# The low halves of the feature-major weights move within their 512-byte frame: 64 bytes in the attention part, 320 in the feed-forward part

## The chip, the cores and the metric

The kernel runs on one core of a Trainium2 chip. The metric is the device time of one execution in microseconds (us), lower is better. Before the change three runs took 1100.12, 1100.26 and 1100.33 us, the median is 1100.26.

Engine names as in the profile: PE is TensorE, PEld its weight loads, DVE VectorE, ACT ScalarE, POOL GpSimd, SP the queue that issues most transfers.

## The reference

One layer of a streaming encoder on 256 tokens of width 2048, all in float32. Only the projections matter here:

```python
def hybrid_mixer(h, w_in_l, ...):
    proj = h @ w_in_l                       # 2048 x 6152
    ...                                     # eight forgetting-attention heads, eight stick-breaking heads
    return merged @ w_out_l                 # 2048 x 2048

def conv_ffn(h, w_up_l, conv_w_l, conv_b_l, w_down_l):
    u = h @ w_up_l                          # 2048 x 11264
    ...                                     # causal depthwise convolution over 3 tokens, split in gate and val
    return (jax.nn.silu(gate) * val) @ w_down_l      # 5632 x 2048
```

## The kernel before

**Three products for one.** The kernel keeps float32 accuracy by splitting each operand into a high part (rounded to the matmul's reduced format, F32R) and a low part (the rest), and adds three products: high times high, high times low, low times high. Weights stream from memory in tiles of 128 x 2048 floats (w_raw). `split` (L217) turns each into w_hi with a copy on ACT (L229) and w_lo with a subtraction on DVE (L232). Tokens are split once and stay: hT[k] holds, for 128 features, 256 high columns and then 256 low columns, so one row of hT[k] is 512 floats, 2048 bytes.

**Two ways to multiply.** A matmul on PE has a stationary operand of 128 x 128, brought in by a weight load, and a moving operand that streams past it. In the *token-major* products (`in_three`, L246, used by `token_major`, `in_seven`, `down_in_seven`; `down_plain` has a loop of its own) the tokens are stationary and the weights move. In the *feature-major* products (`from_features`, L275) it is the other way round: a block of 128 x 128 of the weights is stationary and the tokens move. There a weight tile holds eight blocks of rows and two of columns, so it gives 16 high products and 16 low ones:

```python
hi[:, i, j * P : (j + 1) * P], hT[k].rearrange("p a b -> p (a b)")    # high: 512 moving columns
lo[:, i, j * P : (j + 1) * P], hT[k][:, 0, :]                         # low: the 256 high columns of the tokens
```

`feature_major` (L297) does this for queries and keys of the stick-breaking heads (8 column groups of two halves each), `up_pieces` (L1160) for the whole up-projection (44 column groups of two halves each). That makes 104 weight tiles and 1664 low products. In the attention part and in the first part of the feed-forward layer the second half of a column group does its low products first, so that two groups of 16 low products meet there.

**Addresses.** Every tile has a fixed place in the core's memory, the same in all 128 partitions. One stationary block is 128 floats, 512 bytes, of a partition; the blocks of a feature-major weight tile lie 512 bytes apart and those of the tokens 2048. So within a group of products the place of weights and tokens modulo 512 never changes. In the program as built, hT stands at 96 modulo 512. The pools of w_hi and w_lo of the attention part (two buffers each for w_hi and w_lo) stand at 352, those of the feed-forward part (three each) at 96. Below, *distance* is the address of the stationary operand minus that of the moving one, modulo 512: in the feature-major products it is 256 in the attention part and 0 in the feed-forward part, for high and low alike.

**What sets the order.** PE, DVE, ACT, SP and POOL run the feed-forward layer in an order that is written by hand (L1346): transfers are issued 6 steps ahead of the matmuls, sums 4, splits 2. In the attention part only PE's order is by hand; weights are loaded and split with a raised priority (`weights`, L239).

Of the kernel before, what the change touches and what calls it, by code (L numbers as in the profile page):

```python
# [10 lines left out]
F32R = mybir.dt.float32r  # L11
# [4 lines left out]
P = 128  # L16
# [30 lines left out]
def hybrid_layer(  # L47
# [160 lines left out]
    def load(src):  # L208
        raw = wraw.tile([P, 2048], F32, name="w_raw", tag="w_raw")
        a, b = src.shape[1:]  # L210
        loaded.append(nc.sync.dma_start(raw[:, : a * b].rearrange("p (a b) -> p a b", a=a), src))
        return raw
# [1 line left out]
    loaded = []  # L214
    ordered, last_split = [False], []

    def split(raw, a, b):  # L217

        raws = raw if isinstance(raw, list) else [raw]
        hi = whi.tile([P, 2048], F32R, name="w_hi", tag="w_hi")  # L220
        lo = wlo.tile([P, 2048], F32R, name="w_lo", tag="w_lo")
        n = a * b
        m = n // len(raws)
        with ExitStack() as turn:
            for ins in last_split if ordered[0] else ():
                turn.enter_context(tc.issue_after(ins.ins))
            for i, r in enumerate(raws):
                some = slice(i * m, (i + 1) * m)
                copied = act.copy(hi[:, some], r[:, :m])  # L229
            for i, r in enumerate(raws):  # L230
                some = slice(i * m, (i + 1) * m)
                rest = dve.tensor_tensor(lo[:, some], r[:, :m], f32(hi[:, some]), op=ALU.subtract)  # L232
        last_split[:] = [copied, rest]
        return (
            hi[:, :n].rearrange("p (a b) -> p a b", a=a),
            lo[:, :n].rearrange("p (a b) -> p a b", a=a),
        )

    def weights(src, a, b):  # L239
        with tc.high_priority(offset=AHEAD):  # L240
            return split(load(src), a, b)

    def rows_of(w, k0, n, c0, cols):
        return w[k0 * P : (k0 + n) * P, c0 : c0 + cols].rearrange("(k p) c -> p k c", p=P)
# [30 lines left out]
    def from_features(acc, parts, kh, n=8, low_first=False):  # L275

        hi, lo = parts

        def high(k, i, j):
            nc.tensor.matmul(  # L280
                acc[:, j, :], hi[:, i, j * P : (j + 1) * P],
                hT[k].rearrange("p a b -> p (a b)"), start=k == 0, stop=low_first and k == KT - 1,
            )

        def low(k, i, j):
            nc.tensor.matmul(  # L286
                acc[:, j, S:], lo[:, i, j * P : (j + 1) * P], hT[k][:, 0, :],
                start=False, stop=not low_first and k == KT - 1,
            )

        for i0 in range(0, 8, n):
            for product in (low, high) if low_first else (high, low):
                for i in range(i0, i0 + n):
                    for j in range(2):
                        product(8 * kh + i, i, j)

    def feature_major(w, c0, pool, tag):  # L297

        acc = pool.tile([P, 2, 512], F32, name="pu", tag=tag)
        for kh in range(2):  # L300
            from_features(acc, weights(rows_of(w, 8 * kh, 8, c0, 2 * P), 8, 2 * P), kh, low_first=kh == 1)
            step()
        return acc

# [8 lines left out]
    with ExitStack() as actx:  # L313
# [6 lines left out]
        wlo = actx.enter_context(tc.tile_pool(name="wlo", bufs=2))  # L320
# [102 lines left out]
        def opening():  # L423

            acc = psa.tile([P, NT, 512], F32, name="acc", tag="acc")
            pairs = [[(0, 1), (1, 1)]] + [[(0, 2)]] * 7
            raws, parts = [], []

            def load_w(c, which=None, queue=nc.sync):

                if c == len(raws):
                    raw = wraw.tile([P, 2048], F32, name="w_raw", tag="w_raw")
                    raws.extend([raw[:, :1024], raw[:, 1024:]])
                for i, n in [(which, 1)] if which is not None else [(0, 2)]:
                    queue.dma_start(
                        raws[c][:, i * 512 : (i + n) * 512].rearrange("p (a b) -> p a b", a=n),
                        rows_of(wi, 2 * c + i, n, 0, 512),
                    )

            def split_w(c):  # L440
                hi = whi.tile([P, 2048], F32R, name="w_hi", tag="w_hi")
                lo = wlo.tile([P, 2048], F32R, name="w_lo", tag="w_lo")
                parts.append([t[:, :1024].rearrange("p (a b) -> p a b", a=2) for t in (hi, lo)])
                for i, n in pairs[c]:
                    cols = slice(i * 512, (i + n) * 512)
                    if c == i == 0:
                        dve.tensor_copy(hi[:, cols], raws[c][:, cols])
                        for k in range(2):
                            transposed_split(k, ga, 1)
                    elif c == 1:  # L450
                        for j in range(2):
                            half = slice(512 * j, 512 * (j + 1))
                            dve.tensor_copy(hi[:, half], raws[c][:, half])
                        transposed_split(2, ga)
                    else:
                        act.copy(hi[:, cols], raws[c][:, cols])
                    dve.tensor_tensor(
                        lo[:, cols], raws[c][:, cols], f32(hi[:, cols]), op=ALU.subtract
                    )

            def multiply(c, i, n, high):
                hi, lo = (p[:, i : i + n] for p in parts[c])
                order = [(j, l, hi) for j in range(n) for l in range(2)] if high else [(j, 0, lo) for j in range(n)]
                for m, (j, l, r) in enumerate(order):
                    for t in range(NT):
                        nc.tensor.matmul(
                            acc[:, t, :], of_half(hT[2 * c + i + j], l, t), r[:, j, :],
                            start=high and c == i == m == 0, stop=not high and c == 7 and m == n - 1,
                        )

            load_x(0, 2)
            nc.scalar.dma_start(prow[:KT, :], attn_norm[0].rearrange("(n p) -> n p", p=P))
            act.preload_act_table_set("natural_log_exp_and_others")
            load_w(0, 0)
            load_w(0, 1, nc.scalar)
            load_x(2, 2)
            load_w(1, 0, nc.scalar)
            load_w(1, 1)
            load_x(4, 2)
            load_w(2)  # L480
            load_x(6, 2)
            load_w(3)
            load_x(8, 4)
            load_w(4)
            load_x(12, 4)
            load_w(5)
            keep_busy(14)
            columns(ga, prow[:KT, :], KT)
            split_w(0)
            keep_busy(4)  # L490

            def behind(c):
                if c:
                    transposed_split(2 * c + 2, ga)
                split_w(c + 1)

            multiply(0, 0, 1, True)
            multiply(0, 1, 1, True)
            behind(0)
            sums_of_squares(ss1, 0, [0])  # L500
            multiply(0, 0, 1, False)
            multiply(0, 1, 1, False)
            for c in range(1, 8):
                if c < 7:
                    behind(c)
                sums_of_squares(ss1, c // 2, [c % 2])
                if c == 2:
                    load_w(6)
                    load_w(7)
                multiply(c, 0, 2, True)  # L510
                multiply(c, 0, 2, False)
            return acc
# [647 lines left out]
    def up_pieces(part, f0, follows):  # L1160

        c0 = f0 * P + (DFF if follows is val_follows else 0)
        cell = []

        def piece(kh):
            mem = {}

            def loads():
                mem["raw"] = load(rows_of(wu, 8 * kh, 8, c0, 2 * P))

            def prepare():
                mem["parts"] = split(mem["raw"], 8, 2 * P)

            def matmuls():
                if kh == 0:
                    cell.append(psa.tile([P, 2, 512], F32, name="pu", tag="acc"))
                from_features(cell[0], mem["parts"], kh, 8 if c0 else 4, kh == 1 and part.f_lo == 0)

            new_step(loads, None, prepare, matmuls, (lambda: follows(part, cell[0], f0)) if kh else None)

        piece(0)
        yield
        piece(1)
        yield
# [226 lines left out]
```

## Time and profile before

| | |
|---|---|
| time of the runs, median | 1100.26 us |
| the profiled execution's own time | 1099.91 us |
| its span, first to last instruction | 1098.0 us |
| mean granted TensorE clock | 1.000 |
| PE busy | 1092.8 us (100%) |
| PE weight loads busy | 947.6 us (86%) |
| DVE busy | 907.2 us (83%) |
| ACT busy | 721.6 us (66%) |
| high feature-major products (L280) | 1664 |
| low feature-major products (L286) | 1664 |

The span is taken from one profiled execution; the 1.9 us between the span and that execution's time lie outside the first and last instruction. Matmuls are pipelined: a record begins when a product begins and lasts until its last result is out, so records of neighbours overlap, and the time that a product costs is the step from its beginning to the next one's beginning, not its recorded length. A row of the timeline gives the beginning of the first of a merged group and the length until the last one ends; the group's cost is the distance between its beginning and that of the next row.

### The profile page before, as it was taken

How to read it: one execution, taken by the hardware profiler on the slowest of the kernel's cores; microseconds unless marked ns; L12 is line 12 of the kernel's file. 1: busy time of each engine (PE TensorE's matmuls, PEld its weight loads, DVE VectorE, ACT ScalarE, POOL GpSimd, SP SyncE). 2: the span in 40 equal slices, each digit the busy share in tenths (PEclk: the TensorE clock that was granted, in tenths of full speed). 3: DMA queues.
4: the chain of work that ended last, by engine and by line, in shares of the span. 5: the costliest groups of instructions: out<-in, count | busy, mean ns of one | idle time of the engine just before them, and what ended most of it. 6: DMA issues, size and time to landing. Idle time of an engine off the chain costs nothing. (4 is left out here: it accounts for less than half of the span.)

```text
span 1098.0 us, 14881 instructions
## 1 busy us (share of the span) xinstructions
PE 1092.8 (100%) x5844; PEld 947.6 (86%) x5844; DVE 907.2 (83%) x972; ACT 721.6 (66%) x929; POOL 52.8 (5%) x52
## 2 busy tenths in 40 slices
PE   9999999999999999999999999999999999999998
PEld 7998888888888888888888888888888888888887
DVE  5867877877789786789888988889798889889896
ACT  6756565664665566767767776677677677667753
POOL 0020000000000000001010000100000010100010
PEclk9999999999999999999999999999999999999999
DMA  8797655676649396558999697977979698987985
GB/s 289 232 271 222 191 154 153 197 241 202 207 124 288 118 318 192 187 180 229 278 233 273 194 268 260 260 257 181 326 200 314 197 229 267 263 266 186 320 212 171
DMA packets 182575, 251.15 MB, mean 229 GB/s; under 512 B 4528, under 2 KB 120650, under 8 KB 182250
## 3 DMA queue, kind: packets, MB, share of 16 engines
q1 hardware_dynamic: 162474, 209.67, 57.8%
q0 software_dynamic: 19712, 40.01, 19.7%
q8 instruction: 46, 0.75, 0.3%
q10 hardware_dynamic: 320, 0.53, 0.1%
q14 instruction: 23, 0.19, 0.0%
HBM read 248.08 MB, written 2.11 MB: 228 GB/s over the span
## 5 line engine op out<-in xcount | busy, mean ns | idle before, releaser
L232 DVE TENSOR_TENSOR w_lo<-w_raw,w_hi 128x2048 fp32r<-128x2048 f32 (+1 forms) x192 | 431.8, 2252 | 106.6 <-ACT w_hi L229 106.0
L229 ACT CAST w_hi<-w_raw 128x2048 fp32r<-128x2048 f32 (+1 forms) x192 | 360.9, 1882 | 212.3 <-PE pu L280 59.8
L280 PE MATMUL pu<-hT,w_hi 128*128 128x512 f32 x1664 | 394.0, 390 | 0.0
L280 PEld LDWEIGHTS pu<-hT,w_hi 128*128 128x128 f32 x1664 | 310.3, 188 | 63.1
L286 PEld LDWEIGHTS pu<-hT,w_lo 128*128 128x128 f32 x1664 | 211.9, 191 | 7.0
L286 PE MATMUL pu<-hT,w_lo 128*128 128x256 f32 x1664 | 215.2, 283 | 0.0
L254 PE MATMUL acc<-w_hi,hT 128*128 128x512 f32 (+1 forms) x512 | 113.5, 374 | 0.0
L254 PEld LDWEIGHTS acc<-w_hi,hT 128*128 128x128 f32 x512 | 91.5, 188 | 14.2
L232 DVE TENSOR_TENSOR w_lo<-w_sum,w_hi 128x2048 fp32r<-128x2048 f32 (+1 forms) x38 | 84.2, 2216 | 20.2 <-ACT w_hi L229 20.1
L229 ACT CAST w_hi<-w_sum 128x2048 fp32r<-128x2048 f32 (+1 forms) x38 | 70.3, 1850 | 45.0 <-PE pu L280 35.9
L1106 ACT ACTIVATE tap<-up,ccol 128x256 f32<-128x256 f32 x176 | 74.6, 495 | 0.0
L254 PE MATMUL acc<-w_lo,hT 128*128 128x512 f32 (+1 forms) x256 | 58.9, 372 | 0.0
L1211 POOL DMA_DIRECT2D w_sum<-in_w_down_dram x20 | 25.7, 1283 | 677.6 <-DVE w_lo L232 663.3
L254 PEld LDWEIGHTS acc<-w_lo,hT 128*128 128x128 f32 x256 | 46.4, 188 | 7.5
L254 PE MATMUL bank_a<-w_hi,g 128*128 128x512 f32 x160 | 40.1, 392 | 0.1
L254 PE MATMUL bank_b<-w_hi,s 128*128 128x512 f32 x160 | 40.0, 392 | 0.0
L254 PE MATMUL bank_a<-w_hi,s 128*128 128x512 f32 x160 | 40.0, 392 | 0.0
L254 PEld LDWEIGHTS bank_a<-w_hi,g 128*128 128x128 f32 x160 | 28.8, 189 | 5.8 <-issue 0.5
L254 PEld LDWEIGHTS bank_a<-w_hi,s 128*128 128x128 f32 x160 | 28.9, 189 | 5.3
L254 PEld LDWEIGHTS bank_b<-w_hi,s 128*128 128x128 f32 x160 | 28.9, 189 | 5.2
L1111 DVE TENSOR_TENSOR gate<-gate,tap 128x512 f32<-128x512 f32 x44 | 30.3, 689 | 2.5 <-ACT tap L1106 0.2
L1111 DVE TENSOR_TENSOR val<-val,tap 128x512 f32<-128x512 f32 x44 | 30.3, 689 | 2.3
(282 smaller groups left out, 1166.5 us busy)
## 6 DMA issues: line engine op xcount, KB each, us to landing
w_raw<-in_w_up_dram SPq DMA_DIRECT2D x88, 1024.0 KB, 6.8
w_raw<-in_w_down_dram SPq DMA_DIRECT2D x44, 1024.0 KB, 7.1
w_raw<-in_w_in_dram SPq DMA_DIRECT2D x36, 1024.0 KB, 5.5
w_sum<-in_w_down_dram POOLq DMA_DIRECT2D x20, 1024.0 KB, 9.7
w_raw<-in_w_out_dram SPq DMA_DIRECT2D x14, 1024.0 KB, 5.4
w_raw<-in_w_down_dram POOLq DMA_DIRECT2D x10, 1024.0 KB, 14.8
w_raw<-in_w_in_dram SPq DMA_DIRECT2D x10, 688.0 KB, 4.4
w_raw<-in_w_in_dram SPq DMA_DIRECT2D x6, 512.0 KB, 7.0
```

The source lines that it names most:

```text
L229: copied = act.copy(hi[:, some], r[:, :m])
L232: rest = dve.tensor_tensor(lo[:, some], r[:, :m], f32(hi[:, some]), op=ALU.subtract)
L254: nc.tensor.matmul(o, lhs(i, l, t), r[:, i, :], start=starts and j == 0, stop=stops and j == 3 * n - 1, skip_group_check=more,)
L280: nc.tensor.matmul(acc[:, j, :], hi[:, i, j * P : (j + 1) * P], hT[k].rearrange("p a b -> p (a b)"), start=k == 0, stop=low_first and k == ...
L286: nc.tensor.matmul(acc[:, j, S:], lo[:, i, j * P : (j + 1) * P], hT[k][:, 0, :], start=False, stop=not low_first and k == KT - 1,)
L1106: act.activation(taps[w][:, j, :], u[:, j, w : w + S], AF.Copy, scale=ccol[:, w, f : f + 1])
L1111: dve.tensor_tensor(a, a, tap, op=ALU.add)
L1211: nc.gpsimd.dma_start(mem[into][:, : nk * 512].rearrange("p (a b) -> p a b", a=nk), src, accum_op=ALU.add)
```

## The change

The buffers of w_lo grow from 2048 to 2176 columns (from 8192 to 8704 bytes, 16 and 17 times 512), and `split` takes a start column within them. The attention part's feature-major products ask for column 16 (64 bytes), the up-projection for column 80 (320 bytes); all other users stay at column 0. Since 8704 is a multiple of 512, every other buffer of the kernel keeps its address modulo 512. The low weights of the feature-major products then stand at 416 in both parts, which is a distance of 320 from the tokens at 96. Their high weights stay at distances of 256 and 0. The program has the same instructions in the same order on each engine, with the same waits; what differs is the address that DVE writes for w_lo and that PE reads for it.

```diff
+    LO_COLS = 2048 + 128
+
-    def split(raw, a, b):
+    def split(raw, a, b, lo0=0):
...
-        lo = wlo.tile([P, 2048], F32R, name="w_lo", tag="w_lo")
+        lo = wlo.tile([P, LO_COLS], F32R, name="w_lo", tag="w_lo")[:, lo0:]
...
-    def weights(src, a, b):
+    def weights(src, a, b, lo0=0):
         with tc.high_priority(offset=AHEAD):
-            return split(load(src), a, b)
+            return split(load(src), a, b, lo0)
...
-            from_features(acc, weights(rows_of(w, 8 * kh, 8, c0, 2 * P), 8, 2 * P), kh, low_first=kh == 1)
+            from_features(acc, weights(rows_of(w, 8 * kh, 8, c0, 2 * P), 8, 2 * P, 16), kh, low_first=kh == 1)
...
-                lo = wlo.tile([P, 2048], F32R, name="w_lo", tag="w_lo")
+                lo = wlo.tile([P, LO_COLS], F32R, name="w_lo", tag="w_lo")
...
-                mem["parts"] = split(mem["raw"], 8, 2 * P)
+                mem["parts"] = split(mem["raw"], 8, 2 * P, 80)
```

## The prediction

> **What bounds the kernel now.** I read first the page's busy times, then who PE waited for, then the timeline of one feature-major weight tile, then the recorded lengths of the products that the change touches, and last the other products in the kernel whose operands stand at other distances.
>
> The page's first part, busy time, share of the span and instructions, and from its fifth part the two groups of feature-major products (busy time, mean length of a record, idle time before them):
>
> ```profile
> span 1098.0 us, 14881 instructions
> PE 1092.8 (100%) x5844; PEld 947.6 (86%) x5844; DVE 907.2 (83%) x972; ACT 721.6 (66%) x929; POOL 52.8 (5%) x52
> ...
> L280 PE MATMUL pu<-hT,w_hi 128*128 128x512 f32 x1664 | 394.0, 390 | 0.0
> ...
> L286 PE MATMUL pu<-hT,w_lo 128*128 128x256 f32 x1664 | 215.2, 283 | 0.0
> ```
>
> PE is busy throughout, and neither group of products has idle time before it. The list of waits on PE is just this (in total, times, longest, in us):
>
> ```profile
> PE idle L419 <- DVE zeros L409: 1.1, 1, 1.1
> PE acc L466 <- ACT hT L154: 0.2, 1, 0.2
> ```
>
> PE waits 1.3 us in all, both times at the start. The kernel is therefore bound by the rate at which PE gets through its products; a nanosecond per product is paid or gained in full. In the stretch from 440 to 1050 us (us, then busy time of PE, its weight loads, DVE, ACT and POOL, granted clock, share of the transfer engines, GB/s):
>
> ```profile
> 440.00:1050.00 610.00, 610.00 (x3288) 530.01 (x3287) 533.85 (x474) 429.88 (x481) 34.90 (x27) 1.00 0.85 243
> ```
>
> DVE is free for 610.0 - 533.9 = 76 us of it and ACT for 180, so the engines that feed PE have a margin. The timeline of one weight tile (beginning, length, engine, line):
>
> ```profile
> 516.48 3.79 PE L280 MATMUL pu<-hT,w_hi 128*128 128x512 f32 x16
> 520.11 2.08 PE L286 MATMUL pu<-hT,w_lo 128*128 128x256 f32 x16
> 522.02 0.40 PE L254 MATMUL bank_a<-w_hi,s 128*128 128x512 f32 x1
> ```
>
> From beginning to beginning, 16 high products took 520.11 - 516.48 = 3.63 us, 227 ns each, and 16 low ones 522.02 - 520.11 = 1.91 us, 119 ns each. The low products in all take about 1664 x 119.4 = 199 us, 18% of the time. Their recorded lengths (shortest, median, longest in ns, weight loads first):
>
> ```profile
> L286 PEld LDWEIGHTS pu<-hT,w_lo x1664: 187/192/193, 152.3 to 1049.7; 128*128 128x128 f32 x185
> L286 PE MATMUL pu<-hT,w_lo x1664: 277/283/365, 152.6 to 1049.8; 128*128 128x256 f32 x185
> ```
>
> The median, 283, goes with the steady step of 120 ns. The shortest, 277, is that of the first product of a group, whose step is 113. A longer stall shows in the record one for one, so I use differences of recorded lengths as differences of steps.
>
> **The change, part by part.** *What goes and comes.* No instruction: order and waits are the same on all five engines. 242 writes of w_lo on DVE and the reads of w_lo on PE get new addresses; modulo 512 only those of the 104 feature-major tiles, 104 writes and 1664 products, are new. Larger buffers shift what lies behind them by multiples of 512; no wait changes by it.
>
> *The writes on DVE.* No row shows a write of w_lo at 416. The group is
>
> ```profile
> L232 DVE TENSOR_TENSOR w_lo<-w_raw,w_hi 128x2048 fp32r<-128x2048 f32 (+1 forms) x192 | 431.8, 2252 | 106.6 <-ACT w_hi L229 106.0
> ```
>
> I take no cost. The cover is DVE's 76 idle us between 440 and 1050 us: of the 104 writes 88 belong to the up-projection and most of them lie there, so each would have to grow by some 0.9 us, 40% of its 2.25, before PE waited. A write that gets shorter gains nothing either.
>
> *The 1664 low products.* The only term of the sum is their step at distance 320 in place of 0 and 256. These two are alike: at distance 256, in the attention part, sixteen took 154.48 - 152.57 = 1.91 us as well.
>
> ```profile
> 152.57 2.07 PE L286 MATMUL pu<-hT,w_lo 128*128 128x256 f32 x16
> 154.48 0.28 PE L793 MATMUL ps_o<-pT,vA 128*128 128x256 f32 x1
> ```
>
> The nearest row has the same shape, 256 moving columns, the same kind of data, and exactly this distance: in the attention heads L793 multiplies vA, stationary at 160 modulo 512, with pT, moving at 352, and 160 - 352 is 320 modulo 512. vB and vBlo stand at 224, so their distance is 384:
>
> ```profile
> L793 PE MATMUL ps_o<-pT,vA x24: 277/281/369, 134.1 to 206.6; 128*128 128x256 f32 x24
> ...
> L793 PE MATMUL ps_o<-w,vB x16: 274/284/367, 230.6 to 323.6; 128*128 128x256 f32 x16
> ...
> L793 PE MATMUL ps_o<-w,vBlo x8: 281/284/285, 230.9 to 323.7; 128*128 128x256 f32 x8
> ```
>
> At distance 320 the median is 281, against 283: 2 ns less. (The long ones of each group follow another kind of product and are not steady.) The timeline says the same of three in a row, 134.49 - 134.14 = 0.35 us, 117 ns each:
>
> ```profile
> 134.14 0.52 PE L793 MATMUL ps_o<-pT,vA 128*128 128x256 f32 x3
> 134.49 0.27 PE L794 MATMUL ps_o<-pT,vA_rest 128*128 128x128 f32 x1
> ```
>
> Against this speak products of another shape, 344 moving columns, where the weights move and summed tokens are stationary at 352. Rows of weights there begin 1376 bytes apart, so the distance changes within one tile. The mean over two products at the first row (weights at 352, distance 0), and two at the third (weights at 32, distance 320), around 87.7 and 88.3 us:
>
> ```profile
> L254 PE MATMUL bank_a<-w_hi,hT_sums 128*128 128x344 f32 x2 | 0.5, 316 | 0.0
> ```
>
> ```profile
> L254 PE MATMUL bank_a<-w_hi,hT_sums 128*128 128x344 f32 x2 | 0.5, 321 | 0.0
> ```
>
> Here distance 320 costs 5 ns more than distance 0. So the bounds for a low product are 277 - 283 = -6 ns below (the shortest that a low product itself shows) and +5 ns above. I take -2, from the row with the same number of columns, the same roles and the same distance; its weakness is that only three such products ever follow each other, where the change has 16.
>
> *Skill against row.* The Trainium skill says in "SBUF — State Buffer", section "Who interferes with whom", that TensorE has two read ports, one for the moving operand and one for weights, and that "PE and ACT never wait on anyone"; by that no address matters and the sum is 0. The two rows above, 316 and 321 ns for products that differ in nothing but their addresses, do not fit it.
>
> *The sum.* About 100 of the 1664 products open a group with a record of 277 already; at 281 they lose 4 ns, 0.4 us. The other 1564 gain 2 ns, 3.1 us. Net -2.7 us on the profiled execution's own 1099.91 us, 1097.2. The runs' median is 0.35 us above that execution, so the forecast is 1097.5 us. PE does not wait for DVE or ACT sooner by it: a tile's 16 low products shrink by 0.03 of 1.91 us.
>
> **The rivals.**
>
> *Nothing changes (address has no part in it).* For it: distances 0 and 256 give the same step. Against it: 316 and 321. Time: 1100.3. It is also what the Trainium skill's rule above would give. That the change does not do what it says is excluded by the addresses of the built program.
>
> *The stall goes for all 16.* The first product of each group shows that 256 columns can follow each other at 277 ns of record; if 320 keeps that up, 1564 products gain 6 ns, 9.4 us: 1090.9; with steps of 113 against 120 for them, 10.9 us, 1089.4. For it: the weight loads in the steady low groups are 192 ns long, 4 longer than the median of 188 in the vA row below, so something there holds both streams up. Against it: the vA row itself stays at 281.
>
> ```profile
> L793 PEld LDWEIGHTS ps_o<-pT,vA x24: 187/188/192, 133.9 to 206.4; 128*128 128x128 f32 x24
> ```
>
> *Slower: the weight load runs into the moving stream.* The reads of the next weights fall on the same part of the memory as those of the moving tokens, not at once but some way into the product, and hold them up for longer, as in the 344-column rows. It decides as soon as the step of a steady low product passes 120 ns. At the whole 5 ns the loss is 1664 x 5 = 8.3 us, 1108.6; at half of it 4.2 us, 1104.4. For it: same distance, same engine, and long runs. Against it: the other rows in that tile begin at other places too, and the roles are exchanged.
>
> **How the numbers follow.** A measurement of this kernel can tell about 0.2%, 2.2 us, from no change. Forecast 0.38: since its 2.7 us lie close to that bound, I put 0.25 of it on faster and 0.13 on within. Stall gone 0.20, faster. Nothing 0.14, within. Slower 0.28. Faster 0.45, within 0.27, slower 0.28. The range goes from 1089.4, the stall gone, to 1107.0, which leaves out the upper part of the slower case (about 0.13) and a little below. The forecast's own range, with 1 to 3 ns in place of 2, is 1096.0 to 1098.7.
>
> **What would show it.** Right: the median record of the low products falls from 283 to about 281, that of their weight loads from 192 to 188, sixteen of them take 1.88 to 1.89 us in the timeline, the high products keep 227 ns and 390, PE still waits 1.3 us. Wrong: a median of 283 (nothing), of 277 (stall gone) or of 285 and above (slower). It would also be wrong if the products that follow a low group changed their step; I leave these at nothing, since their own distances stay.

## The result and the profile after

The kernel after takes 1097.27 us (median of 8 runs, 1096.45 to 1098.09); the kernel before took 1100.34 us beside it (8 runs, 1099.83 to 1101.19). The ratio is 0.9971, with a 95% interval from 0.9961 to 0.9982: 0.29% faster, 0.18 to 0.39%. The forecast was 1097.5 us, the range 1089.4 to 1107.0.

The page of the kernel after, the lines that answer to those shown of before (all lines of the code stand two further down, so L288 is the low product and L282 the high one):

```profile
span 1094.7 us, 14881 instructions
PE 1089.0 (99%) x5844; PEld 944.8 (86%) x5844; DVE 907.0 (83%) x972; ACT 721.8 (66%) x929; POOL 52.8 (5%) x52
...
L282 PE MATMUL pu<-hT,w_hi 128*128 128x512 f32 x1664 | 393.9, 390 | 0.0
...
L288 PE MATMUL pu<-hT,w_lo 128*128 128x256 f32 x1664 | 212.2, 282 | 0.0
```

PE's busy time went down by 3.8 us and the span by 3.3. PE waits 1.9 us, where it was 1.3, all of it before the first moved product. DVE and ACT did the same work in the same time, so the write of w_lo at its new place cost nothing that shows. Recorded lengths of the low products' weight loads and of the products (shortest, median, longest):

```profile
L288 PEld LDWEIGHTS pu<-hT,w_lo x1664: 187/188/193, 152.5 to 1046.8; 128*128 128x128 f32 x185
L288 PE MATMUL pu<-hT,w_lo x1664: 275/282/369, 152.7 to 1046.9; 128*128 128x256 f32 x185
```

The weight loads' median fell from 192 to 188 ns, that of the products from 283 to 282. The same place in the program as in the prediction, sixteen low products and what follows them:

```profile
519.01 2.05 PE L288 MATMUL pu<-hT,w_lo 128*128 128x256 f32 x16
520.90 2.00 PE L256 MATMUL bank_a<-w_hi,s 128*128 128x512 f32 x8
522.74 1.07 PE L256 MATMUL bank_a<-w_lo,s 128*128 128x512 f32 x4
```

From beginning to beginning 520.90 - 519.01 = 1.89 us, where it was 1.91. The eight products behind them take 522.74 - 520.90 = 1.84 us, as before:

```profile
522.02 2.00 PE L254 MATMUL bank_a<-w_hi,s 128*128 128x512 f32 x8
523.86 1.07 PE L254 MATMUL bank_a<-w_lo,s 128*128 128x512 f32 x4
```

Ten nanoseconds are too coarse for steps that differ by two, so for the comparisons below I add up the step from the beginning of each PE record to the next, over three kinds of products: all 1664 low ones; the eight products that follow each low group, of whatever kind; and the high ones that are not among those eight. In us:

| kernel | distance of low / high | low | next eight | other high | span |
|---|---|---|---|---|---|
| before | 0, 256 / 0, 256 | 199.37 | 170.85 | 328.68 | 1098.0 |
| after | 320 / 0, 256 | 196.31 | 170.93 | 328.61 | 1094.7 |

The low products gained 199.37 - 196.31 = 3.06 us, which is the change of the span but for 0.24. The other two kinds moved by less than 0.1 us.

### The profile page after: what moved, and what is told of

It is laid out like the page before. It is cut to its first block, busy times and chain, and to the rows that moved or that the text cites. A ratio compares the mean times of both kernels' runs of the same rounds, so it can differ in the third digit from the quotient of the medians.

```text
span 1094.7 us, 14881 instructions
## 1 busy us (share of the span) xinstructions
PE 1089.0 (99%) x5844; PEld 944.8 (86%) x5844; DVE 907.0 (83%) x972; ACT 721.8 (66%) x929; POOL 52.8 (5%) x52
## 4 chain that ended last, share of the span: by engine, by line
PE 99%; DMA 0%; DVE 0%; SPq 0%; issue 0%
PE pu L282 35%; PE acc L256 19%; PE pu L288 18%; PE bank_a L256 12%; PE bank_b L256 6%; PE bank_c L256 3%; PE acc L468 2%; PE acc L1291 1%; PE ps_x L149 1%; PE ps_o L795 1%; PE bank_a L1291 1%; PE ps_p L811 0%; DMA w_raw<-in_w_in_dram 0%; PE ps_o L796 0%; PE ps_h L335 0%; PE ps_s L562 0%
## 5 line engine op out<-in xcount | busy, mean ns | idle before, releaser
L282 PE MATMUL pu<-hT,w_hi 128*128 128x512 f32 x1664 | 393.9, 390 | 0.0
L282 PEld LDWEIGHTS pu<-hT,w_hi 128*128 128x128 f32 x1664 | 310.4, 188 | 62.9
L288 PEld LDWEIGHTS pu<-hT,w_lo 128*128 128x128 f32 x1664 | 209.0, 189 | 6.8
L288 PE MATMUL pu<-hT,w_lo 128*128 128x256 f32 x1664 | 212.2, 282 | 0.0
```

The source lines that it names most:

```text
L282: nc.tensor.matmul(acc[:, j, :], hi[:, i, j * P : (j + 1) * P], hT[k].rearrange("p a b -> p (a b)"), start=k == 0, stop=low_first and k == ...
L288: nc.tensor.matmul(acc[:, j, S:], lo[:, i, j * P : (j + 1) * P], hT[k][:, 0, :], start=False, stop=not low_first and k == KT - 1,)
```

## The experiments

The theory, argued and not seen directly in any trace: each weight load reads its 512 bytes while the tokens of the product before it still stream past, and how often the two hold each other up depends on their distance. Rivals: the place of w_lo itself counts, not its distance from the tokens; or the larger buffers count; or the gain belongs to any place other than 0 and 256. Twelve kernels were run. Each but the last had one run, beside one of the kernel before, and a profile; the table holds what their profiles show.

| kernel | distance of low / high | low | next eight | other high | span | run, beside before |
|---|---|---|---|---|---|---|
| pad_only | 0, 256 / 0, 256 | 199.37 | 170.84 | 328.68 | 1098.9 | 1100.91, 1100.28 |
| all32 | 320 / 0, 256 | 196.31 | 170.94 | 328.61 | 1095.0 | 1097.00, 1099.89 |
| d64 | 64 / 0, 256 | 196.32 | 170.94 | 328.61 | 1095.2 | 1097.11, 1100.28 |
| d192 | 192 / 0, 256 | 196.31 | 172.91 | 328.79 | 1098.1 | 1100.16, 1100.28 |
| d288 | 288 / 0, 256 | 197.16 | 172.09 | 329.52 | 1097.6 | 1099.67, 1099.89 |
| d336 | 336 / 0, 256 | 197.59 | 172.45 | 329.51 | 1099.8 | 1101.62, 1100.42 |
| d352 | 352 / 0, 256 | 195.77 | 170.79 | 328.87 | 1094.8 | 1096.78, 1100.42 |
| d384 | 384 / 0, 256 | 200.35 | 169.52 | 329.20 | 1098.2 | 1100.23, 1100.28 |
| hi320 | 0, 256 / 320 | 199.13 | 171.50 | 338.06 | 1107.4 | 1109.42, 1099.89 |
| hi384 | 0, 256 / 384 | 199.10 | 171.17 | 337.81 | 1107.8 | 1109.88, 1100.42 |
| tm_low | 320 / 0, 256 | 196.31 | 170.94 | 329.89 | 1099.9 | 1101.89, 1099.89 |
| tail384 | 320, last four 384 / 0, 256 | 196.40 | 170.37 | 328.67 | 1094.5 | 1096.39, 1100.00 |

The first feature-major product begins between 148.7 and 150.1 us in these kernels, and none but tm_low changes a distance so far forward; single times and spans therefore carry more than 1 us that has nothing to do with the distance, and the sums of steps are the better measure.

### The larger buffers alone, and the distance kept at another place

pad_only keeps the 2176 columns and puts every user at column 0:

```diff
-            from_features(acc, weights(rows_of(w, 8 * kh, 8, c0, 2 * P), 8, 2 * P, 16), kh, low_first=kh == 1)
+            from_features(acc, weights(rows_of(w, 8 * kh, 8, c0, 2 * P), 8, 2 * P, 0), kh, low_first=kh == 1)
...
-                mem["parts"] = split(mem["raw"], 8, 2 * P, 80)
+                mem["parts"] = split(mem["raw"], 8, 2 * P, 0)
```

> The larger low buffers alone, all at column 0, so distances 0 and 256 as before. If the distance is the cause, everything is as before: 283 ns of record, 120 ns per steady low product, a span of 1098 us. If the larger buffers (what lies behind them moved by 512 to 1536 bytes) bring the gain, 281 ns and 1095 us.

```profile
L288 PEld LDWEIGHTS pu<-hT,w_lo x1664: 187/192/193, 153.6 to 1050.9; 128*128 128x128 f32 x185
L288 PE MATMUL pu<-hT,w_lo x1664: 277/283/365, 153.8 to 1051.0; 128*128 128x256 f32 x185
```

192 and 283 again, as before, and the same three sums within 0.01 us. The buffers' size is not the cause. The span of pad_only is 0.9 us above that of before; its first low product begins at 153.8 us, where before it was 152.6, so this comes from the opening.

all32 moves everything behind the constants by 32 bytes, tokens and weights together:

```diff
+    const.tile([P, 8], F32, name="pad32")
```

> The kernel after, with everything from the constants on moved by 32 bytes: tokens at 128 modulo 512, low weights at 448, every distance as in the kernel after. If the distance is the cause, nothing changes: 118 ns per low product, 227 per high one, a span of 1094.7 us. If the place itself matters (tokens that begin on a multiple of 64 bytes, or weights at 416), the steps of low and high products change.

```profile
L289 PEld LDWEIGHTS pu<-hT,w_lo x1664: 187/188/192, 152.3 to 1046.6; 128*128 128x128 f32 x185
L289 PE MATMUL pu<-hT,w_lo x1664: 276/281/369, 152.5 to 1046.7; 128*128 128x256 f32 x185
```

Same sums as the kernel after, 196.31, 170.94 and 328.61: the low weights stand at 448 here, the tokens at 128, and only relative places are the same. So a relative place is the cause, and the rival of the place itself has fallen. all32 keeps the low weights' distance to the high ones as well as to the tokens; hi320 below changes the first alone (w_hi goes from 96 or 352 to 416, w_lo stays) and leaves the low products at 199.13 us, against 199.37 before. So it is the distance from the tokens that counts.

### Other distances for the low weights

These differ from the kernel after in the two start columns alone:

```diff
# start columns of w_lo in the attention part and in the up-projection
-    16, 80      # after, 320
+    80, 16      # d64
+    112, 48     # d192
+    8, 72       # d288
+    20, 84      # d336
+    24, 88      # d352
+    32, 96      # d384
```

> Low feature-major weights at distance 64 from the tokens, not 320. If the loads and the moving tokens meet in a memory that repeats every 256 bytes (distances 0 and 256 were alike, 120 ns), a steady low product keeps the 118 ns that it has at 320, and the span stays near 1094.7 us. If only the distance modulo 512 counts, or the low weights' own place (416), the step may be anything between 113 and 126 ns: 113 would take 8 us off, 126 would add 13.

d64 gives 196.32, 170.94 and 328.61, the kernel after to 0.01 us. With 0 and 256 alike before, this is the second pair 256 apart that agrees; for these products the distance counts modulo 256.

> Distance 192. If any distance other than 0 and 256 gives what 320 gives: 118 ns, 1094.7 us. If the low weights must be read just ahead of the tokens, as at 64 and 320, this place, where the tokens are 64 bytes ahead modulo 256, should lose the gain: 120 ns or more, 1098 us or more.

Both answers were half right. The low products have exactly the gain of 320, 196.31 us. But the span is that of before, since the products behind the group pay for it, 172.91 against 170.85 us in the next eight and about 1 us more in products still further on, which the table does not hold. The timeline of d192, and then of the eight behind a group in d384:

```profile
519.45 2.05 PE L288 MATMUL pu<-hT,w_lo 128*128 128x256 f32 x16
521.33 2.03 PE L256 MATMUL bank_a<-w_hi,s 128*128 128x512 f32 x8
523.20 1.08 PE L256 MATMUL bank_a<-w_lo,s 128*128 128x512 f32 x4
```

```profile
520.59 2.08 PE L288 MATMUL pu<-hT,w_lo 128*128 128x256 f32 x16
522.51 1.99 PE L256 MATMUL bank_a<-w_hi,s 128*128 128x512 f32 x8
524.33 1.07 PE L256 MATMUL bank_a<-w_lo,s 128*128 128x512 f32 x4
```

The sixteen take 1.88 us at 192 and 1.92 at 384; the eight behind them, whose operands stand the same in all these kernels, take 1.87 and 1.82 us, where before and after have 1.84. Their single steps, from the records' beginnings in one group each (ns):

| | steps of the eight behind a low group |
|---|---|
| before | 233, 236, 228, 233, 231, 226, 227, 227 |
| d192 | 241, 238, 233, 236, 224, 231, 235, 229 |
| d384 | 232, 231, 227, 226, 227, 227, 226, 227 |

A steady step is 226.7 ns. So a low group leaves something behind that takes several products to settle, 28 ns in all before the change and 10 at 384; at 192 it is 53 ns, and 10 more in the two products after these eight (232 and 231). These are the usual groups. Of the 87 with ten products of 512 columns behind them, all take 27 or 28 ns before; at 384, 73 take 9 to 11 and the rest 16 to 29, and at 192, 73 take 53 or 54 and the rest 10 to 43. Nine of the rest are places where two low halves meet and 32 low products follow each other, so what is left behind depends on more than the distance.

> Distance 384. By the vB rows (274 to 284 ns of record, three in a row, median 284) a low product takes between 112 and 121 ns; a median of 284 would mean 120 to 121 and the span of before, 1098 us. If any distance other than 0 and 256 gives what 320 gives, 118 ns and 1094.7 us.

At 384 a low product goes through steps of 118, 120 and 122 ns in turn, 120 on average, as the median of the vB rows had it. The shorter settling (-1.3 us in the next eight) pays for the longer group (+1.0), the high ones lose 0.5, and the span stays as before.

> Distance 288, half of the way from 256 to 320. If the memory's unit is 64 bytes, this is either as at 256 (120 ns, 1098 us) or as at 320 (118 ns, 1094.7 us). If the step depends finely on the distance, it lies between or outside.

> Low weights at distance 336, 16 bytes from 320. If the memory's unit is 32 or 64 bytes, as at 320: 118 ns, 1094.7 us. If it is 16 bytes or less, another step, between 113 and 122 ns.

> Low weights at distance 352, between 320 (118 ns and 28 ns lost in the products behind each group) and 384 (120 ns, 10 ns lost behind). If both vary smoothly: 119 ns and about 19 ns, a span of 1096 us. If they do not: anything from 1093 to 1100 us.

At 288 the low products gain 2.2 us against before, and the next eight and the high ones lose 2.1 together. At 336, only 16 bytes from 320, they gain 1.8 and the others lose 2.4: 0.65 us slower than before by the three sums. At 352 they gain most of all distances, 3.6 us (steps between 115 and 120 ns), and those behind stay as they were; against the kernel after that is 0.4 us in the three sums, too little for a single run to tell. The effect changes within 16 bytes, and neither the step nor the settling is smooth in the distance.

### The high weights, and the low ones that move

hi320 and hi384 leave w_lo at column 0 with 2048 columns and give the larger buffers and the start columns to w_hi:

```diff
+        hi = whi.tile([P, HI_COLS], F32R, name="w_hi", tag="w_hi")[:, hi0:]
-        lo = wlo.tile([P, LO_COLS], F32R, name="w_lo", tag="w_lo")[:, lo0:]
+        lo = wlo.tile([P, 2048], F32R, name="w_lo", tag="w_lo")
```

> The high feature-major weights at distance 320, the low ones back at 256 and 0. If the distance acts alike on every product with stationary weights, a steady high product falls from 226.7 to about 224.7 ns, 1664 x 2 = 3.3 us off: span about 1094.7 us. If a product with 512 moving columns reacts like the 344-column ones (5 ns longer at 320 than at 0), 232 ns and 8 us more: 1106 us. The low products should be back at 120 ns.

> The high feature-major weights at distance 384, the low ones at 256 and 0. At 320 the high products went from 226.7 to 233.6 ns on average. If 0 and 256 are the best places for 512 moving columns, 384 is worse too: over 227 ns, 1099 us of span or more. If 384 suits them (after low products at 384 the high ones settled sooner), under 226 ns, 1096 us or less.

```profile
L282 PE MATMUL pu<-hT,w_hi 128*128 128x512 f32 x1664 | 404.2, 396 | 0.0
```

```profile
519.36 3.90 PE L282 MATMUL pu<-hT,w_hi 128*128 128x512 f32 x16
523.09 2.08 PE L288 MATMUL pu<-hT,w_lo 128*128 128x256 f32 x16
```

The first row is the group in hi320, the second pair its timeline: sixteen high products take 523.09 - 519.36 = 3.73 us, 233 ns each in place of 227. The single steps alternate between 236 and 231 ns. The same distance that takes 2 ns off a product with 256 moving columns puts 6 on one with 512. At 384 it is as bad, with steps from 228 to 241. For the high weights 0 and 256 are the better places of those tried.

tm_low starts from the kernel after and moves the low weights of the token-major products to column 48, so that the stationary tokens are 64 or 320 from the moving weights:

```diff
-    def split(raw, a, b, lo0=0):
+    def split(raw, a, b, lo0=48):
...
-    def weights(src, a, b, lo0=0):
+    def weights(src, a, b, lo0=48):
```

> The kernel after, with the low weights of the token-major products moved too: there the weights move and the tokens are stationary, and the distance becomes 64 or 320 in place of 0 or 256. About 640 low products with 512 columns take part. If these gain 2 ns like the feature-major ones, 1.3 us less than after, 1093.4 us of span; if they react like the 344-column rows (5 ns longer), 3 us more, 1098 us.

Three groups of token-major products, first in the kernel after, then in tm_low, the first with 512 moving columns, then the few at the end with 256 (w_lo moved, w_hi did not):

```profile
L256 PE MATMUL bank_b<-w_lo,s 128*128 128x512 f32 x80 | 21.4, 389 | 0.0
...
L1291 PE MATMUL bank_a<-w_hi,g 128*128 128x256 f32 x16 | 2.2, 283 | 0.0
...
L1291 PE MATMUL bank_a<-w_lo,g 128*128 128x256 f32 x8 | 1.3, 283 | 0.0
```

```profile
L256 PE MATMUL bank_b<-w_lo,s 128*128 128x512 f32 x80 | 21.9, 394 | 0.0
...
L1291 PE MATMUL bank_a<-w_hi,g 128*128 128x256 f32 x16 | 2.2, 281 | 0.0
...
L1291 PE MATMUL bank_a<-w_lo,g 128*128 128x256 f32 x8 | 1.3, 281 | 0.0
```

The low products with 512 columns lose 5 ns of record (steps of 233.3 in place of 226.7). The eight with 256 columns show 2 ns less, but so do the sixteen high ones beside them, which did not move, and the steps of the low ones run from 114 to 122 ns: groups of four do not show a steady step, so this gain cannot be put down to their own distance. With 512 columns, then, the distance costs time whether tokens (here) or weights (hi320) are stationary and whether the moved weights are low or high. With weights stationary, 512 columns lose and 256 gain. What is left to turn the sign is the number of moving columns; that is a conclusion by exclusion, as no run changes the number of columns alone. The high products that follow such a group pay as well (329.89 against 328.61 us). The span is 5.2 us above that of the kernel after, where the slower answer had 3.

### What a group leaves behind

tail384 starts from the kernel after and puts rows 6 and 7 of the eight in a low tile 64 bytes further on, at distance 384, so that a group spends twelve products at 320 and ends with four at 384. DVE writes such a tile in two pieces.

```diff
+                for c0, c1, shift in ((0, 1536, 0), (1536, m, 16)) if lo0 else ((i * m, i * m + m, 0),):
+                    rest = dve.tensor_tensor(
+                        lo[:, c0 + shift : c1 + shift], r[:, c0 - i * m : c1 - i * m], f32(hi[:, c0:c1]), op=ALU.subtract
+                    )
...
+            [lo[:, k * b + 16 * (k > 5) :][:, :b] for k in range(a)] if lo0 else lo[:, :n].rearrange("p (a b) -> p a b", a=a),
```

> The kernel after, with the last four of each tile's 16 low products at distance 384 and the first twelve at 320; DVE writes each such tile in two pieces (1536 and 512 columns). If the extra time of the products behind a low group is set by where the group's last products stood, it falls from 28 ns a group (at 320) to 10 (at 384), while the low products stay near 118 ns: 1.9 us less than after, 1095.4 us, ratio to before 0.9955. If the whole group sets it, or the change of distance inside the group costs as much, 1097 us or more. The second DVE piece is hidden: PE waits for nothing new.

```profile
518.88 2.06 PE L291 MATMUL pu<-hT,w_lo 128*128 128x256 f32 x16
520.77 1.99 PE L259 MATMUL bank_a<-w_hi,s 128*128 128x512 f32 x8
522.60 1.07 PE L259 MATMUL bank_a<-w_lo,s 128*128 128x512 f32 x4
```

The eight behind the group now take 236, 233, 227, 226 ns and then the steady step: 16 ns to settle, in place of 28 and of the 10 that were expected. The last five low products take 122, 120, 119, 115 and 120 ns, 596 in all, where the same group of the kernel after has 590. The sum over the three kinds is 0.41 us below the kernel after (the low products +0.09, the next eight -0.56, the high ones +0.06). The end of a group does set what the next products pay, but four products do not reach the state that sixteen at 384 reach. Nor does every group gain: of 87 as above, 72 take 16 or 17 ns and 15 take 42 or 43, more than in the kernel after, nine of them behind 32 low products in a row. That is why the sum falls by 0.56 us and no more. Over 7 runs the kernel takes a median of 1096.39 us against 1100.00 before, a ratio of 0.9970 (0.9959 to 0.9982). That beats before; it cannot be told from the kernel after at 0.9971.

## Why the prediction was right

- *The bound.* PE's rate, and nothing that waits: 3.06 us saved in the low products gave 3.3 us of span. Right. The sign that PE would still wait 1.3 us did not hold to the letter: it waits 1.9 us, still before the first moved product.
- *The term of the sum.* The step of a low product, -2 ns for 1564 of them and 4 ns more for the first of each group, -2.7 us. Measured -3.06 us: 199.37 to 196.31 over 1664 products, 119.8 to 118.0 ns. The first of a group did lose its short step (118 or 119 in place of 113 or 114 in single up-projection groups), and the last one takes 120 or 121. The median record came out at 282 where 281 was foreseen; all32 and d64 show 281 with the same sums. The rule that differences of records are differences of steps holds only to some 3 ns: at 192 the median record is 279 with the same 118.0 ns per product, and the token-major products of tm_low have 5 ns more of record for 6.6 of step. The forecast did not need it, since the three vA products take 117 ns each by their beginnings too. The forecast's own range is summed unevenly: with a gain of 1 ns and 5 ns lost by the first of each group its upper end is 1099.2, not 1098.7.
- *The row it rested on.* The vA products, three at a time, told the steady step of sixteen. The 344-column rows, which spoke against it, do not show what was read from them. The low products of the same rows of weights have the same distances, and they come out in the reverse order. Here are the two at distances 0 and 160, and then the two at 320 and 480, around 88.9 and 89.3 us in the trace of before:

```profile
L254 PE MATMUL bank_a<-w_lo,hT_sums 128*128 128x344 f32 x2 | 0.5, 323 | 0.0
```

```profile
L254 PE MATMUL bank_a<-w_lo,hT_sums 128*128 128x344 f32 x2 | 0.5, 318 | 0.0
```

At distance 0 the high products have 316 ns and a low one 323; at 320 they have 321 and 318. So the 316 and 321 cannot be put down to the distance, and they were no evidence against the rival that nothing changes; what else acts there is open. To give these rows the smaller weight was right. The reason given for it, the number of columns, fits 256 and 512 columns at this distance (512 lose 5 ns of record in tm_low and 6 in the mean of hi320); that products of 512 columns would lose was not to be known from these rows.

- *The rival that nothing changes* has fallen: the low products moved by 3.06 us, and in hi320 high products with unchanged work take 233 in place of 227 ns by an offset of their weights. The Trainium skill's "SBUF — State Buffer", section "Who interferes with whom", has it that PE and ACT never wait on anyone and that PE's two read ports are independent; these runs disagree with what the prediction drew from that, that no address matters.
- *The stall gone for all sixteen* did not come: no distance tried has a mean step below 117.6 ns (195.77 us over 1664 products, at 352).
- *The slower rival* came about for other products, those with 512 columns: 233 in place of 227 ns in hi320. Its mechanism is not shown.
- *What I left at nothing* was nothing at 320, the products behind a group: 170.93 against 170.85 us. That was not earned by an argument. At 192, 288 and 336 the same step would have failed, since there these products take 1 to 2 us more and eat the gain.

What stays open is what the two streams share. The runs show that for the low products the place of the weights relative to the tokens decides (all32, with hi320), that this repeats after 256 bytes (d64, and 0 with 256), that 16 bytes matter (d336), and that weight loads of the steady groups are 4 ns longer at 0 and 256 (192 against 188). The loads do not tell the step, though: at 384 their median is 189 with a step of 120 ns. That reads of weights and of moving columns meet in the same part of the memory fits the relative place and the repeat; it was argued, not shown, and it explains neither the sign at 512 columns nor the settling.

## What to carry to other kernels

When PE is the bound and never waits, look at the step from one product's beginning to the next: a few nanoseconds, the same for thousands of products, are worth moving an operand by some bytes within its frame. Try the distance on each shape of product by itself, since the same distance helped 256 moving columns and harmed 512, and count the products behind the group as well. Look first for rows of the same shape that already stand at another distance in the same trace; three of them were enough here.

## What was not expected of the hardware

- A group's distance changes the steps of products behind it that have not moved: between 10 ns (384) and 63 ns (192) to settle in the usual groups, over up to ten products.
- Steps need not settle to one value: 118, 120, 122 in turn at 384, 236 and 231 in turn for the high products at 320.
- For 512 moving columns 64 or 320 cost 6.6 ns per product in the token-major low products (226.7 to 233.3), about the same as in the feature-major high ones (6 on average).
